# Hybrid decoder layer on one core: the bias table is stored once per head, and the queries of a block are kept last one first

## Chip, cores and metric

The kernel runs on one core of a Trainium2 chip. The metric is the device time of one execution in microseconds, as the median of several runs; lower is better.

## What is computed

One layer of a decoder with 256 tokens of width 2048, all in float32. The parts that matter here are the attention heads: 6 differential heads (A), 4 block heads (B) and 6 dilated heads (C), each of width 128. Every logit gets a bias that depends on the distance between query and key alone, through a table of 32 buckets and 16 heads:

```
def rel_bias(table, dist):
    return jnp.moveaxis(table.astype(jnp.float32)[t5_bucket(dist)], -1, 0)
...
        dist = qpos[:, None] - kpos[None, :]
        s = jnp.einsum('bhcqd,bhckd->bhcqk', qi, kt).astype(jnp.float32) * scale
        s = s + rel_bias(table, dist)[None, :, None]
        s = jnp.where(dist >= 0, s, NEG_INF)
        p = jax.nn.softmax(s, axis=-1)
```

After the heads come an output projection, a cross attention to 256 memory tokens, and a gated feed-forward part of width 5632. The weights are about 222 MB (212 pieces of 1 MB), each read once.

## The kernel before

**Weights and products.** Each weight matrix is cut into pieces of 1 MB (`raw`, four buffers). SyncE's queue issues the load of a piece (`load`, line 126) as soon as VectorE is done with the buffer that it takes. A piece is worked in two halves: ScalarE casts a half to the rounded type float32r (`split_hi`, line 141, tile `hi`), VectorE takes the difference (`split_lo`, line 148, tile `lo`), and TensorE multiplies with both. The split runs four halves ahead of the products. There are two kinds of products: `wstat_chunk` (lines 264 and 268) has the weights stationary, `astat_chunk` (lines 307 to 309) has the tokens stationary.

**Order.** The order on every engine is written out by hand. The program counts halves; `before(i, f)` and `after(i, f)` hang other work on half i, ahead of VectorE's split of it or behind TensorE's products of it. Heads run in this way beside the products: scores, softmax, transposes and the product with the values are spread over some ten halves. The last lines of the kernel walk through all halves and issue what hangs on them.

**The bias.** `setup_small`, hung on half 14, makes on TensorE and VectorE one row of 384 values for each head (tile `s`, called `rev` in the code): the bias of the distances 255, 254 and so on. GpSimd's queue then stores it to DRAM (line 967), in the tensor `bias_dram`. `load_bias` (line 355) reads for a head a tile `bias` of 128 queries by 256 keys, in which each query's row is shifted by one against the row above. It is issued six halves ahead of the head's scores, on SyncE's queue, between loads of weights. `biased` (line 399) adds it to the scores.

**Queries.** `merge_to` (line 336) writes the transposed queries and keys of a head (tile `qk`) with the factor of the norm, `copied` (line 417) takes the transposed probabilities out of PSUM (tile `pt`) for the product with the values.

Of the kernel before, what the change touches and what calls it, by code (L numbers as in the profile page):

```python
# [11 lines left out]
F32 = mybir.dt.float32  # L12
F32R = mybir.dt.float32r
AF = mybir.ActivationFunctionType
ALU = mybir.AluOpType
AX = mybir.AxisListType

P = 128
D = 2048
S = 256  # L20
NT = 2
KD = D // P
# [18 lines left out]

# First distance of each relative-position bucket that distances 0..255 reach.
BUCKET_AT = list(range(17)) + [22, 30, 40, 54, 73, 99, 134, 182, 246]
RL = 384


def bias_constants():
    """By shape alone: the bucket of the distance 255 - i, one-hot, and what each head group adds to it."""
    dist = 255 - np.arange(RL)
    bucket = np.searchsorted(np.array(BUCKET_AT), np.maximum(dist, 0), side="right") - 1  # L50
    onehot = np.zeros((NBUCK, RL), np.float32)
    onehot[bucket, np.arange(RL)] = dist >= 0
    add = np.full((NH, RL), NEG, np.float32)
    add[: HA + HB, dist >= 0] = 0.0
    times = (dist <= 128).astype(int) + (dist % 4 == 0) + (dist % 16 == 0)
    seen = (dist >= 0) & (times > 0)
    add[HA + HB :, seen] = np.log(times[seen].astype(np.float64)).astype(np.float32)
    return onehot, add
# [3 lines left out]
def trunk(ctx, tc, x, mem, w_in, w_out, g_mix, diff_lambda, diff_subln, rel_bias_table, g_cross, g_mem,  # L62
# [25 lines left out]
    def any_tile():  # L88
        """All the banks in turn, where nothing but products needs them."""
        turn[0] += 1  # L90
        return (acc_tile if turn[0] % 8 < NACC else at_tile)()
# [3 lines left out]

    # ---------------------------------------------------------------- loads of weights
    # A piece is 1 MB of a weight matrix, one 8 KB row in each partition; it is split into its two
    # float32r parts in two halves.
    class Piece:
# [51 lines left out]

    # What runs beside the products: `before` what the vector engine does ahead of a half's work, `after`
    # the rest. A value that goes from one engine to another is mostly picked up a half later, so that no
    # engine waits in its queue.
    pre, post = {}, {}
# [11 lines left out]

    # ---------------------------------------------------------------- constants
    ident = cst.tile([P, P], F32, name="ident")
# [5 lines left out]

    # ---------------------------------------------------------------- norms
    def rstd_of(ss, n, width, r=None):
        """(ss / n + eps) ** -0.5 of [P, width] sums of squares."""
        ms = small(width, f"ms{width}")
        DVE.tensor_scalar(ms, ss, 1.0 / n, EPS, op0=ALU.mult, op1=ALU.add)  # L180
        if r is None:
            r = small(width, f"rstd{width}")
        POOL.tensor_tensor(r, ms, mhalf.to_broadcast([P, width]) if width > 1 else mhalf, op=ALU.pow)
        return r

    def put_steps(src, g, dst, c):
        """Transposes 256 columns, src(t) of 128 tokens, of a norm's input, times the gain, into the two
        float32r parts of dst[:, 2c:2c+2, :]; the products take the rows' factor afterwards."""
        st = {}

        def turn():
            st["p"] = at_tile()
            for j in range(2):
                for t in range(NT):
                    o = j * S + t * P
                    PE.transpose(st["p"][:, o:o + P], src(t)[:, j * P:(j + 1) * P], ident)  # L196

        def high():
            for j in range(2):
                k = 2 * c + j  # L200
                ACT.activation(dst()[:, k, :S], st["p"][:, j * S:(j + 1) * S], AF.Copy, scale=gT[:, g, k:k + 1])

        def low():
            for j in range(2):
                k = 2 * c + j
                DVE.scalar_tensor_tensor(dst()[:, k, S:], st["p"][:, j * S:(j + 1) * S], gT[:, g, k:k + 1],
                                         dst()[:, k, :S].bitcast(F32), op0=ALU.mult, op1=ALU.subtract)

        return turn, high, low
# [12 lines left out]
    def norm_factors(i, key, ss):  # L222
        """The norm's factor of each token, from sums [P, (t c)] of squares: in a column and along rows."""
        st = {}
# [24 lines left out]

    # ---------------------------------------------------------------- products  # L250
    def wstat_chunk(w, col0, ncol, src, evac, rows=KD, bank=acc_tile):
        """(src @ w[:, col0:col0+512]).T, 128 columns to a bank: [hi x hi + lo x hi | hi x lo]."""
        accs = [None] * 4
# [34 lines left out]
    def astat_chunk(w, col0, ncol, src, evac, korder):  # L288
        """src @ w[:, col0:col0+ncol], 128 tokens to a bank; korder are blocks of 128 rows of w."""
        accs = [None] * NT  # L290
# [34 lines left out]
    def merge(a):  # L325
        """a[:, :256] + a[:, 256:]."""
        t = tmp.tile([P, S], F32, tag="mg", name="mg", bufs=4)
        ACT.copy(t, a[:, S:])
        DVE.tensor_tensor(t, a[:, :S], t, op=ALU.add)  # L329
        return t  # L330

    def merge_to(n, place, a, scale, key, wait=0):
        """The n-th of four: place() = scale * rows' factor * merge(a)."""
        m = merge(a)
        before(cur[0] + 1 + wait + n // 2,
               lambda: DVE.scalar_tensor_tensor(place(), m, scale, rrow[key], op0=ALU.mult, op1=ALU.mult))

# [3 lines left out]

    # ---------------------------------------------------------------- attention
    qT, kT, vN = {}, {}, {}
# [3 lines left out]
    lam = small(1, "lam", 1)  # L347
    bias_dram = dram.tile([NH, P, RL], F32, name="bias_dram")
    BT = {}

    def load_bias(h):
        BT[h] = pools["att"].tile([P, S], F32, tag="bias", name="bias", bufs=4)
        src = bass.AP(tensor=bias_dram.tensor, offset=bias_dram.offset + h * P * RL + 127,
                      ap=[[RL - 1, P], [1, S]])
        SP.dma_start(BT[h], src)

# [9 lines left out]
    def products(out, a, b, first=True, last=True):  # L366
        """out += a.T @ b, of [high, low] float32r parts."""
        for i, (u, w) in enumerate(((0, 0), (0, 1), (1, 0))):
            PE.matmul(out, a[u], b[w], start=first and i == 0, stop=last and i == 2)  # L369

    def spare(n):
        """Room in the heads' outputs that only the last group fills."""
        return mixed["t"][:, HA + 2 * (n % 2):HA + 2 * (n % 2) + 2, :]
# [20 lines left out]
    def biased(sp, b, nm):  # L394
        """scores + bias of both query blocks into SBUF; minus their maxima into nm."""
        s = pools["att"].tile([P, RL], F32, tag="s", name="s", bufs=3)
# [11 lines left out]
    def transposed(s):  # L408
        """P.T of [q0 x k0 | q1 x k0 | q1 x k1]."""
        pt = at_tile()  # L410
        for j in range(3):
            PE.transpose(pt[:, j * P:(j + 1) * P], s[:, j * P:(j + 1) * P], ident)  # L412
        return pt

    def copied(pt):
        t = pools["att"].tile([P, RL], F32, tag="pt", name="pt", bufs=4)
        ACT.copy(t, pt[:, :3 * P])
        return t
# [163 lines left out]

    # ---------------------------------------------------------------- the program, piece by piece
    # Projections of one group of heads.
    def group(col0, nheads, h0, tag, qscale):
        def put(dst, h, scale):
            def f(n, a):
                dst[h] = pools["att"].tile([P, S], F32, tag="qk", name="qk", bufs=16)
                merge_to(n, lambda: dst[h], a, scale, "x", 5 if cur[0] < KD // 2 else 0)
            return f  # L590
# [40 lines left out]

    # Output projection, with the residual; the memory's norm in between.
    ss1 = small(8, "ss1", 1)
# [68 lines left out]

    # One buffer: the heads' outputs, the transposed weights and the values, each in two parts.
    def new_cross():
# [69 lines left out]

    # Down projection: all banks, every weight once.
    outs = {}
# [88 lines left out]

    # ---------------------------------------------------------------- start
    g4 = pools["att"].tile([P, S], F32, tag="on", name="on", bufs=2)[:4 * KD, :P]
# [41 lines left out]

    # The tensor engine's clock rises with steady work: it turns the identity until the first loads are there.  # L910
    warm = acc_tile()
# [40 lines left out]
    def setup_small():  # L952
# [13 lines left out]
        DVE.tensor_tensor(rev, pr[:NH, :RL], badd, op=ALU.add)  # L966
        POOL.dma_start(bias_dram, rev[:, None, :].to_broadcast([NH, P, RL]))
        pc = at_tile()
# [54 lines left out]
```

## Time and profile before

| what | value |
|---|---|
| median of 3 runs | 1282.57 us (1282.16 to 1284.3) |
| span of the profiled execution, first to last instruction | 1281.3 us |
| mean granted clock of TensorE | 0.991 |
| busy: TensorE, VectorE, ScalarE, GpSimd | 1253.5, 809.3, 629.7, 18.2 us |
| moved by DMA | 236.33 MB, 184 GB/s in the mean |

Of the profiled execution only its span is known, which is 1.3 us shorter than the median. A busy time counts an engine's instructions and none of its waits. The ends of matmuls are modelled, so the distances between their starts tell more than their lengths. The DMA share is the busy share of the sixteen DMA engines in the mean, whatever they move in that time; it can come out slightly above 1.

### The profile page before, as it was taken

What the parts mean: (1) busy time and instruction counts of PE and PEld (TensorE: products, weight loads), DVE (VectorE), ACT (ScalarE), POOL (GpSimd) and SP (SyncE); (2) the same over time, 40 slices, a digit from 0 to 9 for tenths busy, and PEclk for the clock granted to TensorE, in tenths of its full rate; (3) what the DMA queues carried; (4) which work ended last, traced back from release to release, by engine and by line L of the source; (5) the groups of instructions that cost most, each with busy time, mean ns of one, the idle gap of its engine ahead of it and who ended that gap; (6) DMA issues with size and microseconds to landing.
All of it is one profiled execution on the core that took longest, in us unless ns stands there. A gap on an engine that the chain in (4) does not pass through costs nothing.

```text
span 1281.3 us, 17348 instructions
## 1 busy us (share of the span) xinstructions
PE 1253.5 (98%) x6784; PEld 1070.4 (84%) x6784; DVE 809.3 (63%) x1304; ACT 629.7 (49%) x1017; POOL 18.2 (1%) x31
## 2 busy tenths in 40 slices
PE   8969999999999999999999999999999999999997
PEld 7857888888888889888888888888888888888885
DVE  5625677567555577677677677767767765445455
ACT  5514565556455555654444444445444444444444
POOL 1000000000000000000000000000000000000000
PEclk9988999999999999999999999999999999999998
DMA  9697554555456554555555555555555555555541
GB/s 326 206 152 234 173 176 163 188 178 172 158 166 241 174 165 135 214 178 175 200 185 182 204 178 192 178 200 183 184 204 177 190 197 179 182 197 185 180 161 66
DMA packets 106465, 236.33 MB, mean 184 GB/s; under 512 B 4283, under 2 KB 15130, under 8 KB 100624
## 3 DMA queue, kind: packets, MB, share of 16 engines
q1 hardware_dynamic: 105296, 231.75, 53.0%
q0 software_dynamic: 1056, 3.47, 2.4%
q8 instruction: 53, 0.87, 0.3%
q14 instruction: 28, 0.23, 0.1%
q10 hardware_dynamic: 32, 0.01, 0.0%
HBM read 229.97 MB, written 5.24 MB: 184 GB/s over the span
## 4 chain that ended last, share of the span: by engine, by line
issue 58%; PE 36%; DMA 4%; DVE 1%; SPq 0%; POOL 0%; ACT 0%; DVEq 0%; POOLq 0%; ACTq 0%
PE acc L264 10%; PE acc L307 6%; PE acc L308 6%; PE acc L309 6%; PE acc L268 5%; DMA raw<-in_w_in 3%; DMA xbig<-in_x 1%; PE at L369 1%; PE at L196 1%; PE at L388 0%; PE at L412 0%; PE at L440 0%; SPq L136 0%; DVE lo L148 0%; PE at L441 0%
## 5 line engine op out<-in xcount | busy, mean ns | idle before, releaser
L148 DVE TENSOR_TENSOR lo<-raw,hi 128x1024 fp32r<-128x1024 f32 x424 | 518.3, 1224 | 400.2 <-ACT hi L141 399.3
L141 ACT CAST hi<-raw 128x1024 fp32r<-128x1024 f32 x424 | 443.9, 1049 | 487.0 <-PE acc L264 244.5
L264 PE MATMUL acc<-hT,hi 128*128 128x512 f32 x1520 | 539.1, 396 | 0.0
L268 PE MATMUL acc<-hT,lo 128*128 128x256 f32 x1520 | 421.1, 279 | 0.0
L264 PEld LDWEIGHTS acc<-hT,hi 128*128 128x128 f32 x1520 | 284.7, 187 | 66.9
L268 PEld LDWEIGHTS acc<-hT,lo 128*128 128x128 f32 x1520 | 283.9, 188 | 0.3
L264 PE MATMUL at<-hT,hi 128*128 128x512 f32 x528 | 188.6, 393 | 0.0
L307 PE MATMUL acc<-hi,hT 128*128 128x512 f32 (+1 forms) x384 | 140.7, 366 | 13.7 <-DVE mg L329 13.7
L268 PE MATMUL at<-hT,lo 128*128 128x256 f32 x528 | 147.3, 279 | 0.0
L308 PE MATMUL acc<-lo,hT 128*128 128x512 f32 (+1 forms) x384 | 138.3, 360 | 0.0
L309 PE MATMUL acc<-hi,hT 128*128 128x512 f32 (+1 forms) x384 | 138.3, 360 | 0.0
L264 PEld LDWEIGHTS at<-hT,hi 128*128 128x128 f32 x528 | 98.9, 187 | 23.7
L268 PEld LDWEIGHTS at<-hT,lo 128*128 128x128 f32 x528 | 98.9, 187 | 0.0
L307 PEld LDWEIGHTS acc<-hi,hT 128*128 128x128 f32 x384 | 73.0, 190 | 25.0 <-DVE mg L329 14.1
L797 PE MATMUL acc<-lo,ah 128*128 128x512 f32 x220 | 87.2, 396 | 0.0
L796 PE MATMUL acc<-hi,ah 128*128 128x512 f32 x220 | 87.2, 396 | 0.0
L798 PE MATMUL acc<-hi,al 128*128 128x512 f32 x220 | 87.2, 396 | 0.0
L309 PEld LDWEIGHTS acc<-hi,hT 128*128 128x128 f32 x384 | 73.0, 190 | 12.0
L308 PEld LDWEIGHTS acc<-lo,hT 128*128 128x128 f32 x384 | 73.1, 190 | 10.7
L798 PE MATMUL at<-hi,al 128*128 128x512 f32 x132 | 52.3, 396 | 0.0
L796 PE MATMUL at<-hi,ah 128*128 128x512 f32 x132 | 52.3, 396 | 0.0
L797 PE MATMUL at<-lo,ah 128*128 128x512 f32 x132 | 52.3, 396 | 0.0
(159 smaller groups left out, 920.1 us busy)
## 6 DMA issues: line engine op xcount, KB each, us to landing
raw<-in_w_up SPq DMA_DIRECT2D x88, 1024.0 KB, 4.9
raw<-in_w_in SPq DMA_DIRECT2D x45, 1024.0 KB, 5.2
raw<-in_w_down SPq DMA_DIRECT2D x44, 1024.0 KB, 4.9
raw<-in_w_out SPq DMA_DIRECT2D x12, 1024.0 KB, 5.5
raw<-in_w_ckv SPq DMA_DIRECT2D x8, 1024.0 KB, 5.2
raw<-in_w_out SPq DMA_DIRECT2D x8, 512.0 KB, 5.0
raw<-in_w_cq SPq DMA_DIRECT2D x4, 1024.0 KB, 5.3
raw<-in_w_co SPq DMA_DIRECT2D x4, 1024.0 KB, 5.2
```

The source lines that it names most:

```text
L141: ACT.copy(hi, p.raw[:, h * HALF:(h + 1) * HALF])
L148: DVE.tensor_tensor(lo, p.raw[:, h * HALF:(h + 1) * HALF], hi.bitcast(F32), op=ALU.subtract)
L196: PE.transpose(st["p"][:, o:o + P], src(t)[:, j * P:(j + 1) * P], ident)
L264: PE.matmul(accs[n], hi[:, j, n * P:(n + 1) * P], src()[:, k, :], start=(k == 0), stop=False)
L268: PE.matmul(accs[n][:, :S], lo[:, j, n * P:(n + 1) * P], src()[:, k, :S], start=False, stop=(k == rows - 1))
L307: PE.matmul(o, xh, hi[:, j, :], start=(i == 0), stop=False)
L308: PE.matmul(o, xh, lo[:, j, :], start=False, stop=False)
L309: PE.matmul(o, xl, hi[:, j, :], start=False, stop=(i == len(korder) - 1))
L369: PE.matmul(out, a[u], b[w], start=first and i == 0, stop=last and i == 2)
L796: PE.matmul(o, ah, wh, start=(k == 0), stop=False)
L797: PE.matmul(o, ah, wl, start=False, stop=False)
L798: PE.matmul(o, al, wh, start=False, stop=(k == KF - 1))
```

## The change

The tensor `bias_dram` has one row for each head, not one for each query of each head, and the store writes that row once. A row of 384 values is the same for all queries but for its shift. A load can step forwards by one value from partition to partition, where the tile of before steps back by one. So partition p of the tile `bias` now belongs to query 127 - p of its block, and the queries are put in that order: `merge_to` reads its two inputs of each block of 128 backwards when it writes queries, and `copied` reads the transposed probabilities of each block backwards, which restores the order. Keys and values stay as they are. The comments that were removed are left out here.

```
     def merge_to(n, place, a, scale, key, wait=0, order=lambda a: a):
         m = merge(a)
         before(cur[0] + 1 + wait + n // 2,
-               lambda: DVE.scalar_tensor_tensor(place(), m, scale, rrow[key], op0=ALU.mult, op1=ALU.mult))
+               lambda: DVE.scalar_tensor_tensor(place(), order(m), scale, order(rrow[key]), op0=ALU.mult,
+                                                op1=ALU.mult))
...
+    def turned(a):
+        return a.rearrange("p (t n) -> p t n", t=2)[:, :, ::-1]
...
-    bias_dram = dram.tile([NH, P, RL], F32, name="bias_dram")
+    bias_dram = dram.tile([NH, RL], F32, name="bias_dram")
...
-        src = bass.AP(tensor=bias_dram.tensor, offset=bias_dram.offset + h * P * RL + 127,
-                      ap=[[RL - 1, P], [1, S]])
+        src = bass.AP(tensor=bias_dram.tensor, offset=bias_dram.offset + h * RL, ap=[[1, P], [1, S]])
         SP.dma_start(BT[h], src)
...
         t = pools["att"].tile([P, RL], F32, tag="pt", name="pt", bufs=4)
-        ACT.copy(t, pt[:, :3 * P])
+        ACT.copy(t.rearrange("p (j n) -> p j n", j=3), pt[:, :3 * P].rearrange("p (j n) -> p j n", j=3)[:, :, ::-1])
...
+                if dst is qT:
+                    merge_to(n, lambda: t.rearrange("p (t n) -> p t n", t=2), a, scale, "x", late, turned)
+                else:
+                    merge_to(n, lambda: t, a, scale, "x", late)
...
-        POOL.dma_start(bias_dram, rev[:, None, :].to_broadcast([NH, P, RL]))
+        POOL.dma_start(bias_dram, rev)
```

No instruction is added, taken away or moved on TensorE, VectorE, ScalarE and SyncE. On GpSimd, whose rows around the store follow, with those that begin with - for before and + for after, the store alone has another shape: the numbers are rows and values of the transfer.

```order
 L183 TENSOR_TENSOR rcol_x<-ms_501,mhalf 128x2
-L967 DMA bias_dram<-s 2048x1x384
+L977 DMA bias_dram<-s 16x384
 L183 TENSOR_TENSOR rstd_1363<-ms_1361,mhalf 128x2
 L183 TENSOR_TENSOR rstd_1596<-ms_1594,mhalf 128x2
```

The transfer goes from 2048 rows to 16 and stands where it stood; later lines of the file have moved by ten.

## Rows read from the trace of the kernel before

**Rows 1.** The page: the span, and busy time, share and instructions of the engines.

```profile
span 1281.3 us, 17348 instructions
...
PE 1253.5 (98%) x6784; PEld 1070.4 (84%) x6784; DVE 809.3 (63%) x1304; ACT 629.7 (49%) x1017; POOL 18.2 (1%) x31
```

**Rows 2.** Long stretches: length, busy time of each engine, granted clock, DMA share, GB/s.

```profile
160.00:320.00 160.00, 160.00 (x951) 139.50 (x950) 111.21 (x277) 94.43 (x211) 3.45 (x5) 1.00 0.53 176
...
112.00:1264.00 1152.00, 1151.97 (x6250) 985.14 (x6250) 742.92 (x1198) 571.23 (x919) 7.29 (x9) 1.00 0.53 181
```

**Rows 3.** All waits of TensorE: total us, times, longest us.

```profile
PE acc L307 <- DVE mg L329: 13.7, 1, 13.7
PE at L196 <- DMA xbig<-in_x: 3.9, 5, 1.4
PE acc L915 <- POOL mhalf L172: 1.3, 1, 1.3
```

**Rows 4.** The longest wait of another engine in 80 to 98 us.

```profile
ACT hi L141 <- DMA raw<-in_w_in: 18.7, 1, 18.7
```

**Rows 5.** The chain that ended last: start, us, what.

```profile
59.67 34.41 DMA raw<-in_w_in
```

**Rows 6.** DMA in 40 to 56 us: packets, MB, share of 16 engines.

```profile
q1 hardware_dynamic: 1354, 2.70, 52.6%
```

**Rows 7.** The same in 56 to 98 us; then an issue, us to landing.

```profile
q0 software_dynamic: 704, 3.15, 71.3%
q1 hardware_dynamic: 1951, 3.86, 24.0%
...
bias_dram<-s POOLq DMA_DIRECT2D x1, 3072.0 KB, 35.9
```

**Rows 8.** Stretches of 8 us, with the columns of rows 2.

```profile
64.00:72.00 8.00, 8.00 (x48) 6.99 (x47) 3.68 (x3) 2.80 (x4) 0.00 (x0) 1.00 0.97 104
...
80.00:88.00 8.00, 4.31 (x23) 3.34 (x22) 0.00 (x0) 0.00 (x0) 0.00 (x0) 0.93 1.01 137
88.00:96.00 8.00, 0.00 (x0) 0.00 (x0) 0.74 (x1) 1.82 (x2) 0.00 (x0) 0.50 1.00 231
96.00:104.00 8.00, 5.99 (x14) 4.74 (x15) 6.65 (x12) 3.25 (x7) 0.00 (x0) 0.50 1.07 365
```

**Rows 9.** DMA issues of the whole span: count, KB each, median us to landing.

```profile
raw<-in_w_down SPq DMA_DIRECT2D x44, 1024.0 KB, 4.9
...
gfin<-in_g_final SPq DMA_DIRECT2D x1, 1024.0 KB, 6.9
...
s<-in_biasadd POOLq DMA_DIRECT2D x1, 24.0 KB, 7.1
```

**Rows 10.** TensorE in order of time around the gap: start, us, instruction.

```profile
83.21 0.39 PE L309 MATMUL acc<-hi,hT 128*128 128x512 f32 x1
...
83.91 0.40 PE L309 MATMUL acc<-hi,hT 128*128 128x512 f32 x1
...
98.01 0.80 PE L307 MATMUL acc<-hi,hT 128*128 128x512 f32 x1 [13.70 <-DVE mg L329]
...
104.32 0.39 PE L307 MATMUL acc<-hi,hT 128*128 128x512 f32 x1
```

**Rows 11.** The stretch behind the gap, with the columns of rows 2.

```profile
98.00:104.30 6.30, 6.29 (x15) 4.97 (x16) 4.65 (x9) 1.25 (x2) 0.00 (x0) 0.52 1.08 355
```

**Rows 12.** The tile `bias`: ns least/median/most, first and last start.

```profile
L399 DVE CUSTOM_DVE_ANT_0 s<-at,bias x44: 281/356/422, 137.1 to 326.2; 128x128 f32<-128x128 f32 x22, 128x256 f32<-128x256 f32 x22
L355 SPq DMA_DIRECT2D bias<-bias_dram x16: 338/498/901, 110.8 to 302.6; - x16
```

**Rows 13.** The lines 336, 417 and 971, with the columns of rows 12.

```profile
L336 DVE SCALAR_TENSOR_TENSOR qk<-mg,rrow x32: 415/418/422, 49.5 to 306.0; 128x256 f32<-128x256 f32 x32
L417 ACT COPY pt<-at x16: 466/474/492, 146.8 to 337.3; 128x384 f32<-128x384 f32 x16
L971 DVE COPY convT<-at x1: 449/449/449, 58.1 to 58.1; 128x176 f32<-128x176 f32 x1
```

More of the change, by code (lines that the diff above doesn't have):

```diff
@@ L330, in merge, with merge_to @@
         return t
-    def merge_to(n, place, a, scale, key, wait=0):
+    def turned(a):
+        return a.rearrange("p (t n) -> p t n", t=2)[:, :, ::-1]
+    def merge_to(n, place, a, scale, key, wait=0, order=lambda a: a):
         m = merge(a)
         before(cur[0] + 1 + wait + n // 2,
-               lambda: DVE.scalar_tensor_tensor(place(), m, scale, rrow[key], op0=ALU.mult, op1=ALU.mult))
+               lambda: DVE.scalar_tensor_tensor(place(), order(m), scale, order(rrow[key]), op0=ALU.mult,
+                                                op1=ALU.mult))
     def high_low(hi, lo, x, scale=1.0):
@@ L587, in f @@
             def f(n, a):
-                dst[h] = pools["att"].tile([P, S], F32, tag="qk", name="qk", bufs=16)
-                merge_to(n, lambda: dst[h], a, scale, "x", 5 if cur[0] < KD // 2 else 0)
+                dst[h] = t = pools["att"].tile([P, S], F32, tag="qk", name="qk", bufs=16)
+                late = 5 if cur[0] < KD // 2 else 0
+                if dst is qT:
+                    merge_to(n, lambda: t.rearrange("p (t n) -> p t n", t=2), a, scale, "x", late, turned)
+                else:
+                    merge_to(n, lambda: t, a, scale, "x", late)
             return f
```

## Prediction

> **What bounds the kernel now.** I read the busy times first: TensorE is busy 1253.5 of 1281.3 us, and no other engine passes 63% [rows 1]. So only what TensorE executes, or what makes it stand still, sets the time. From 112 to 1264 us it is busy 1151.97 of 1152.00 us at a granted clock of 1.00 [rows 2]: nothing there is to be won without fewer or shorter matmuls, and nothing that another engine does there is on the path as long as it is not late.
>
> The list of waits has one large entry for TensorE: 13.7 us once, at line 307 [rows 3]. The releaser named is VectorE's `mg`; but that instruction merely stood last in VectorE's queue, and what was late is found further back: ScalarE's cast of a weight piece waited 18.7 us for the load of `raw` from `in_w_in` [rows 4], and VectorE's split waits behind that cast. The chain of the end shows the load itself: issued at 59.67 us, landed 34.41 us later [rows 5], where pieces of 1 MB elsewhere land in 4.9 us [rows 9].
>
> What filled the DMA engines is in the queues' shares of 56 to 98 us: the software queue, on which GpSimd stores `bias_dram`, held 71.3% of the sixteen engines' time, the weights' hardware queue only 24.0% [rows 7]. The store is 3072 KB and took 35.9 us to land. Before it the engines were not short: from 40 to 56 us the weights needed 52.6% of them [rows 6]. In the stretches of 8 us the whole story is seen [rows 8]: the DMA share goes to 1.00 while the traffic falls to 104 GB/s, TensorE's work ends in 80 to 88 us, the next stretch has none, and the granted clock is 0.50 there and in the one after.
>
> **The change, part by part.** *The store shrinks.* It writes 16 rows of 384 values in place of 2048, so 24 KB in place of 3072 KB; the lists of instructions differ on no engine except in this one transfer's shape. Its old cost on the engines: 71.3% of 16 x 42 us is 479 engine-us, 0.234 us for each of 2048 rows. Sixteen rows at that price are 3.7 engine-us: 0.23 us if all engines share them, 3.7 us if one engine has them all. The nearest row from the other side is the 24 KB load of `in_biasadd` on the same queue, which took 7.1 us to land in the crowded start [rows 9]. TensorE went on for 24.5 us after the first starved load was issued (59.67 to 84.14 us), on pieces already loaded and already split. Against that cover 0.23, 3.7 and 7.1 us are all hidden: I put the new store at 0, and the stall disappears whole.
>
> What the stall is worth I count from TensorE's own instructions [rows 10]. In steady work three matmuls of 512 columns start in 0.70 us (83.21 to 83.91), 0.234 us each. The last before the gap starts at 83.91, so the next was due at 84.14; it starts at 98.01. That is 13.87 us of standing. After it 15 matmuls start before the one at 104.32 [rows 11], 0.42 us apart in the mean, the pace of the granted clock of 0.50 (1.2 of 2.4 GHz): 6.31 us where 15 x 0.234 = 3.51 would do, so 2.80 us more. Together **16.7 us** (as a check: 104.32 - 83.91 = 20.41 us for 16 matmuls that need 3.75).
>
> The clock part can be had in another way, so I weigh it. By the rows the clock was 0.93, 0.50 and 0.50 in the three stretches of 8 us from 80 to 104 us [rows 8], so at half for 1.1 + 8 + 8 = 17.1 us, but TensorE has matmuls only in its last 6.3 us, and only these are lengthened. The Trainium skill, "TensorE: Matmul & The Clock Gate", section "Terms", prices throttling as the throttled time times one minus the clock ratio: an estimate by that page is 17.1 x 0.5 = 8.6 us in place of 2.8, and a sum of 22.4 us. The rows speak against using it here, since idle time costs the same at either clock; I keep 2.8.
>
> *The stall has no second home, if weights keep landing.* The pieces that follow are used at one in 6.0 us (212 pieces in 1281 us, a half in 3.0 us [rows 1]) and land in about 5 [rows 9]; after 98 us TensorE never waits again [rows 2, 3], and all that follows is the same list of instructions moved 16.7 us earlier.
>
> *The reads of the table.* Each of 16 loads of `bias` still takes 128 rows of 1 KB, but now all 128 lie in the same 1.5 KB of DRAM, one value apart. No row shows this for `bias`; the nearest is the load of `gfin`, which gives every partition the same 8 KB: 6.9 us for 1 MB, against 4.9 us for a piece of `in_w_down` of the same size with rows of its own [rows 9]. So from no change to 1.4 times: 5.0 to 7.0 us. The first load is issued at 110.8 us and its first reader starts at 137.1 [rows 12]: 26.3 us of cover. I put it at 0.
>
> *Reading backwards.* Sixteen products `qk` on VectorE (line 336, 418 ns, 256 values) and sixteen copies `pt` on ScalarE (line 417, 474 ns, 384 values) now walk each block from its end. No row has a negative step. The lower bound is no change. The upper I take from strided work: the copy of `convT`, whose writes are four values apart, takes 449 ns for 176 values, 2.55 ns each, where line 336 takes 1.63 [rows 13]. That is 0.92 ns more: 0.24 us for each product and 0.35 us for each copy, 3.8 and 5.6 us in all. These engines are busy 111 and 94 of 160 us in 160 to 320 us [rows 2], and the parts of a head are a half piece (3.0 us) or more apart in the queue. I put it at 0; were the cover gone, 9.4 us would come back. The Trainium skill, "Vector Engine (DVE) Microarchitecture Reference", section "Measured stream behaviour on trn2", measures up to 2.51 ns a value for small non-adjacent steps and says that a negative step was not measured; an estimate by it is 0.37 us for each product, hidden as well.
>
> **Sum.** Profiled execution: span 1281.3 - 16.7 = 1264.6 us. The median of the runs is 1282.57, 1.3 us above that span; with the same distance the forecast is **1265.9 us**.
>
> **Rivals.**
> *The clock gives back more.* The half clock's cost is 8.6 us, not 2.8, as if the engine would have used all of its 17.1 us: 1282.57 - 22.4 = 1260.2 us. For it is only that one cannot see what the clock would do without the gap; against it are the starts counted above. The Trainium skill, "TensorE: Matmul & The Clock Gate", section "Terms", would have it so. 3 in 100.
> *The backwards reads come to the path.* TensorE's transposes and products of the heads wait for `qk` and `pt`, at the worst for all of 9.4 us: 1275.3 us. For: VectorE's work of a head comes in bursts. Against: TensorE waits for neither anywhere in the profile of before [rows 3]. 3 in 100.
> *The stall stays.* If the weights were late by themselves, the store is innocent and the time is 1282.6. Against: 71.3% in its queue, and 52.6% of use just ahead of it. 2 in 100.
> *Slower.* The loads of `bias` crowd on one spot of DRAM and hold the engines. They come every 12.8 us (15 steps from 110.8 to 302.6 [rows 12]), and the weights use 53% [rows 2], so 6.0 us are free in each step. With the cover of 24.5 us, the gain is gone and 2.6 us more lost when each load holds all engines for 6.0 + (24.5 + 16.7 + 2.6) / 16 = 8.7 us; at 10 us it is 16 x 4.0 - 24.5 - 16.7 = 22.8 us worse, 1305 us. Against: `gfin` reads eight times as many bytes from one spot in 6.9 us from issue to landing. 2 in 100.
>
> **Numbers.** The forecast has 90 in 100. Its range takes 0.4 us below and 1.7 above from the spread of the runs (1282.16 to 1284.3), another 2.5 us below for starts near the gap that are modelled or missing, and 2.4 above for a quarter of the backwards price: 1263 to 1270 us, which leaves out the rivals, together 1 in 10. A change of 0.2% (2.6 us) is about what can be told from none. Faster 0.96 (forecast, clock, backwards), same 0.02 (stall stays), slower 0.02.
>
> **What the profile will show.** Right: no wait of TensorE over 2 us after the start; granted clock 1.00 in every slice from the third on; some 3.1 MB less on the software queue; pieces landing in 5 us between 59 and 95 us; the first matmul at line 307 about 0.23 us behind the one ahead of it. Wrong: `bias` landing in over 8 us; TensorE waiting at the transposes or scores of the heads; lines 336 and 417 much over 0.66 and 0.83 us; or a gap still between 80 and 100 us.

## The result, and the profile after

The changed kernel takes 1266.41 us (median of 4 runs, 1266.02 to 1266.92) against 1282.62 us for the kernel before: a ratio of 0.9872 with a 95% interval of 0.9858 to 0.9886. That is 16.2 us by the medians; the spans of the two profiled executions differ by 16.5 us. The forecast was 1265.9 us.

The page of the changed kernel, span, busy times, granted clock and DMA share in 40 slices:

```profile
span 1264.8 us, 17348 instructions
...
PE 1250.7 (99%) x6784; PEld 1068.6 (84%) x6784; DVE 809.0 (64%) x1304; ACT 630.2 (50%) x1017; POOL 17.7 (1%) x31
...
PEclk9999999999999999999999999999999999999998
DMA  9655554555465454555555565565655555555541
```

The busy times of VectorE and ScalarE are the same to 0.5 us [rows 1]; TensorE is 2.8 us less busy, which is what its matmuls at half clock had been longer. Only the last slice, where the work ends, is below nine tenths of the clock.

All waits of TensorE after, as in [rows 3]:

```profile
PE at L196 <- DMA xbig<-in_x: 3.9, 5, 2.0
PE acc L925 <- POOL mhalf L172: 1.4, 1, 1.4
```

The 13.7 us are gone and nothing has come in their place; the two small waits of the start are as before. The stretches that held the gap [rows 8] have full work at full clock, with the DMA engines busy for 0.45 to 0.75 of the time:

```profile
64.00:72.00 8.00, 8.00 (x48) 6.96 (x47) 3.74 (x4) 2.80 (x4) 0.00 (x0) 1.00 0.45 148
...
80.00:88.00 8.00, 8.00 (x40) 6.64 (x39) 6.08 (x11) 4.45 (x7) 0.00 (x0) 1.00 0.59 195
88.00:96.00 8.00, 8.00 (x36) 6.44 (x35) 3.23 (x4) 3.16 (x3) 0.00 (x0) 1.00 0.51 148
96.00:104.00 8.00, 8.00 (x35) 6.43 (x35) 3.25 (x4) 3.15 (x3) 0.00 (x0) 1.00 0.75 261
```

The DMA queues in 56 to 98 us after, to be laid beside [rows 7], and the issues there with the time to landing:

```profile
q1 hardware_dynamic: 5217, 8.33, 60.6%
...
q0 software_dynamic: 32, 0.02, 0.2%
...
raw<-in_w_in SPq DMA_DIRECT2D x7, 1024.0 KB, 5.2
bias<-bias_dram SPq DMA_DIRECT2D x1, 128.0 KB, 5.0
bias_dram<-s POOLq DMA_DIRECT2D x1, 24.0 KB, 1.8
```

The store lands in 1.8 us in place of 35.9, and the pieces beside it land in 5.2 us. At the place of the old gap, where the second bank of the first value product begins, TensorE goes on 0.24 us after the matmul ahead of it:

```profile
84.12 0.40 PE L309 MATMUL acc<-hi,hT 128*128 128x512 f32 x1
84.36 0.39 PE L307 MATMUL acc<-hi,hT 128*128 128x512 f32 x1
```

### The profile page after: what moved, and what is told of

Read it like the earlier page. It is cut to its first block, busy times and chain, and to the rows that moved or that the text cites. A ratio compares the mean times of both kernels' runs of the same rounds, so it can differ in the third digit from the quotient of the medians.

```text
span 1264.8 us, 17348 instructions
## 1 busy us (share of the span) xinstructions
PE 1250.7 (99%) x6784; PEld 1068.6 (84%) x6784; DVE 809.0 (64%) x1304; ACT 630.2 (50%) x1017; POOL 17.7 (1%) x31
## 4 chain that ended last, share of the span: by engine, by line
issue 58%; PE 39%; DMA 1%; SPq 0%; DVE 0%; POOL 0%; ACT 0%; DVEq 0%; POOLq 0%; ACTq 0%
PE acc L264 11%; PE acc L307 6%; PE acc L309 6%; PE acc L308 6%; PE acc L268 6%; DMA xbig<-in_x 1%; PE at L375 1%; PE at L196 1%; PE at L394 0%; PE at L418 0%; PE at L446 0%; SPq L136 0%; PE at L447 0%; SPq L885 0%; POOL raw L820 0%
```

## Experiments

Each is compared with the kernel before, run beside it; where a small difference matters the interval is given.

**The old store with the queries turned.** One part of the change is undone. The load of a head begins at the head's first row, as it must in the larger tensor (left out here); it still steps forwards.

```
-    bias_dram = dram.tile([NH, RL], F32, name="bias_dram")
+    bias_dram = dram.tile([NH, 128, RL], F32, name="bias_dram")
...
-        POOL.dma_start(bias_dram, rev)
+        POOL.dma_start(bias_dram, rev[:, None, :].to_broadcast([NH, 128, RL]))
```

> The changed kernel with the queries turned, but with the old store of 128 equal rows per head (3072 KB). If the store alone made the time: 1282.6 us within 2, the store landing in about 36 us, one wait of TensorE of 13.7 us near 84 us and half clock behind it. If the backwards order has a price of its own, up to 9.4 us more than that; if the order of the queries (and not the store) gave the gain, 1266 us. Lines 340 and 423 take 418 and 472 ns as in the changed kernel either way.

Measured: 1282.56 us, ratio 1.0001 (0.9992 to 1.0011). The store lands in 36.1 us, lines 340 and 423 take 422 and 472 ns in the median, and TensorE's list of waits has its large entry again:

```profile
PE acc L307 <- DVE mg L329: 14.1, 1, 14.1
```

So the whole gain is the store's; the order of the queries alone gives nothing and costs nothing, to within the 0.1% of that interval.

**Plain order with the small store.** Here the backwards reads are taken out, and each query gets another one's bias.

```
-                    merge_to(n, lambda: t.rearrange("p (t n) -> p t n", t=2), a, scale, "x", late, turned)
+                    merge_to(n, lambda: t, a, scale, "x", late)
...
-        ACT.copy(t.rearrange("p (j n) -> p j n", j=3), pt[:, :3 * P].rearrange("p (j n) -> p j n", j=3)[:, :, ::-1])
+        ACT.copy(t, pt[:, :3 * P])
```

> The changed kernel with the small store and the new loads, but queries in plain order: the two backwards reads are taken out, so each query gets the bias of another one. If backwards reads cost nothing: 1266.4 us within 1, lines for qk and pt at 418 and 472 ns. If they had a hidden price on the path: 1260 to 1265 us.

Measured: 1266.41 us, the same median as the changed kernel. The two lines first in the changed kernel (nanoseconds least, median, most):

```profile
L340 DVE SCALAR_TENSOR_TENSOR qk<-mg,rrow x32: 411/418/422, 49.7 to 289.5; 128x256 f32<-128x256 f32 x32
L423 ACT COPY pt<-at x16: 470/472/494, 130.3 to 320.9; 128x384 f32<-128x384 f32 x16
```

and then in this one:

```profile
L340 DVE SCALAR_TENSOR_TENSOR qk<-mg,rrow x32: 415/419/423, 49.5 to 289.3; 128x256 f32<-128x256 f32 x32
L423 ACT COPY pt<-at x16: 469/472/491, 130.1 to 320.7; 128x384 f32<-128x384 f32 x16
```

Half of the 32 products and all 16 copies read backwards in the first and none in the second, and the medians differ by 1 ns at most, less than the 4 ns by which line 340 differs between executions: a step of minus one in float32 costs nothing on these engines here.

**Less of the store.** The two kernels store 96 and 64 equal rows for each head, in place of 1 (and of 128 before); but for the tensor's shape and the load's start, which follow, they are the changed kernel. With 96:

```
-        POOL.dma_start(bias_dram, rev)
+        POOL.dma_start(bias_dram, rev[:, None, :].to_broadcast([NH, 96, RL]))
```

> The changed kernel with 96 equal rows per head stored (2304 KB). If the DMA engines' time is the cause, the store lands in about 27 us, the first starved piece with it at 85 to 86 us, and TensorE stands some 5 us in place of 13.9; with 0 to 2.8 us for the clock that is 1271 to 1275 us. If any big store costs the same stall (a fixed wait, or its start): 1282 us. If the cover of 24.5 us held in full against the 27 us: 2 to 3 us of standing, 1269.

> The changed kernel with 64 equal rows per head stored (1536 KB). By the engines' time the store lands in about 18 us, under the cover of 24.5 us: no wait of TensorE, clock 1.00, 1266.4 us within 1. If the loss goes in proportion to the bytes: half of 16.7 us, 1275 us.

Measured: 1275.22 us with 96 rows, 1266.41 us with 64. The stores landed in 27.5 and 18.6 us, as the engines' time has it. With 64 rows TensorE waits nowhere near the place, so the loss does not go with the bytes: it begins past a threshold, which lies between 18.6 and 27.5 us to landing. With 96 rows it stands:

```profile
83.65 0.40 PE L309 MATMUL acc<-hi,hT 128*128 128x512 f32 x1
87.19 1.99 ACT L141 CAST hi<-raw 128x1024 fp32r<-128x1024 f32 x2 [11.96 <-DMA raw<-in_w_in]
88.27 2.36 DVE L148 TENSOR_TENSOR lo<-raw,hi 128x1024 fp32r<-128x1024 f32 x2 [11.79 <-ACT hi L141]
89.09 1.19 ACT L328 COPY mg<-acc 128x256 f32<-128x256 f32 x4
...
90.55 1.41 DVE L329 TENSOR_TENSOR mg<-acc,mg 128x256 f32<-128x256 f32 x4
91.02 0.79 PE L307 MATMUL acc<-hi,hT 128*128 128x512 f32 x1 [6.97 <-DVE mg L329]
...
95.26 0.39 PE L308 MATMUL acc<-lo,hT 128*128 128x512 f32 x1
```

That is 7.1 us of standing where I expected some 5. The piece, issued at 59.4 us, lands 27.7 us later, at 87.1, where I expected it at 85 to 86; from there a cast, two splits and the first of the four sums `mg` still go ahead of TensorE's first matmul, 3.8 us (87.19 to 91.02). The ten matmuls that start ahead of the one at 95.26 take 4.24 us, where 2.34 would do at full clock; 7.1 and 1.9 make 9.0 us, against 8.8 by the medians.

**A free bank for the waiting product.** The rows above name not the weights but `mg`. In the kernel before, only the second bank of PSUM of the first value product is taken from the other ring, which is idle there.

```
-                        accs[t] = acc_tile()
+                        accs[t] = (at_tile if cur[0] == 24 and t else acc_tile)()
```

> The kernel before, with one edit: the second bank of PSUM of the first value product (half 24) comes from the other, idle ring of banks, so that TensorE needn't wait until VectorE has emptied a bank of the product ahead. If TensorE stood for that bank, as the list of waits names it, it goes on with the 18 matmuls whose halves are split (4.2 us), and starts again at about 96.5 us when the next half is split: 5.7 us less, 1276.9 us, the wait then named by the weights' tiles. If it stood for the weights, as my prediction read it: 1282.6 us.

Measured: 1276.71 us, ratio 0.9957 (0.9940 to 0.9974). TensorE goes on until the split halves are used up:

```profile
83.91 0.39 PE L307 MATMUL at<-hi,hT 128*128 128x512 f32 x1
...
87.89 0.39 PE L309 MATMUL at<-hi,hT 128*128 128x512 f32 x1
94.23 1.99 ACT L141 CAST hi<-raw 128x1024 fp32r<-128x1024 f32 x2 [18.99 <-DMA raw<-in_w_in]
95.31 2.36 DVE L148 TENSOR_TENSOR lo<-raw,hi 128x1024 fp32r<-128x1024 f32 x2 [18.81 <-ACT hi L141]
95.33 0.80 PE L307 MATMUL acc<-hi,hT 128*128 128x512 f32 x1 [7.05 <-ACT hi L141]
```

The 18 matmuls run ahead of the gap, and the wait is now 7.05 us and for the weights. So in the kernel before TensorE stood for the bank: its emptying was queued, on ScalarE and VectorE, behind casts and splits that waited for the late piece, while one and a half split halves lay ready. The rows of the kernel before show that queue; TensorE's matmul at 98.01 us [rows 10] starts when the first of the four sums `mg` is done:

```profile
94.18 1.99 ACT L141 CAST hi<-raw 128x1024 fp32r<-128x1024 f32 x2 [18.70 <-DMA raw<-in_w_in]
95.26 2.36 DVE L148 TENSOR_TENSOR lo<-raw,hi 128x1024 fp32r<-128x1024 f32 x2 [18.52 <-ACT hi L141]
96.08 1.19 ACT L328 COPY mg<-acc 128x256 f32<-128x256 f32 x4
...
97.54 1.41 DVE L329 TENSOR_TENSOR mg<-acc,mg 128x256 f32<-128x256 f32 x4
```

**Work in the gap.** Transposes of the identity are put where TensorE of the kernel before stands, to see what the half clock costs.

```
+                    if cur[0] == 24 and t == 0:
+                        fill = at_tile()
+                        for _ in range(210):
+                            PE.transpose(fill[:, :P], ident, ident)
```

> The kernel before, with 210 additional transposes of the identity (about 12 us, their result is not used) at the place where TensorE stands still. If only the matmuls behind the gap are lengthened by the half clock: the clock stays at 1.00 and the time is 1282.6 - 2.8 = 1279.8 us. If the half clock costs half of its 17.1 us: 1274.0 us. If the transposes take longer than the gap: more than 1282.6.

Measured: 1289.98 us. The transposes took 22.85 us (84.80 to 107.65), longer than the gap, so the third case came and the time by itself does not part the first two; but they kept the clock up, as the stretches behind the rows of TensorE show:

```profile
84.80 17.41 PE L313 MATMUL at<-ident 128*128 128x128 f32 x158
...
107.65 0.47 PE L307 MATMUL acc<-hi,hT 128*128 128x512 f32 x1
```

```profile
88.00:96.00 8.00, 8.00 (x76) 8.00 (x75) 0.00 (x0) 0.00 (x0) 0.00 (x0) 1.00 0.99 204
96.00:104.00 8.00, 8.00 (x75) 8.00 (x74) 6.16 (x11) 4.04 (x7) 0.00 (x0) 1.00 1.07 372
```

In place of the gap and the half clock there are 22.85 us. If those two cost 13.87 + 2.80 us, the span grows by 6.2 us; if they cost 13.87 + 8.6, by 0.4. It grew by 6.9 (1288.2 against 1281.3), of which 0.66 us had come up before the place was reached (the first value matmul starts at 83.41, in the kernel before at 82.75). That leaves 6.2; by the medians the time grew by 7.3 us.

> The filler again, with 115 transposes in place of 210, since 210 took 22.85 us (0.109 us each): 12.5 us, inside the gap of 13.9 us. If only the matmuls behind the gap are lengthened by the half clock: clock 1.00 through the gap, 1282.6 - 2.8 = 1279.8 us. If the half clock costs half of its 17.1 us: 1274.0 us. If the clock is of no account: 1282.6 us.

Measured: 1282.56 us in the median of ten, 1281.63 without the tenth, ratio 0.9994 (0.9985 to 1.0004): inconclusive. In the profiled execution, one of 1283.82 us, the late piece came some 2 us later than before (its cast starts at 96.21 us, not at 94.18), so the filler ended 2.48 us too soon and the clock fell once more for a short time:

```profile
84.84 12.72 PE L313 MATMUL at<-ident 128*128 128x128 f32 x115
100.03 0.51 PE L307 MATMUL acc<-hi,hT 128*128 128x512 f32 x1 [2.48 <-DVE mg L333]
```

Five executions took 1280.29 to 1281.63 us, near the first theory, and four 1283.48 to 1284.08. The tenth took 2530.35 us, for which I have no explanation.

**What made the store slow.** In the changed kernel a further store of 3072 KB, whose result is not used, is put behind the small one: the same number of rows of the same length on the same queue, but read from 128 partitions.

```
+    wide_dram = dram.tile([P, NH, RL], F32, name="wide_dram")
...
+        POOL.dma_start(wide_dram, xbig[:, 0:1, :RL].to_broadcast([P, NH, RL]))
```

> The changed kernel with an additional store of 3072 KB at the same place and on the same queue, of the same 2048 rows of 1536 bytes, but read from all 128 partitions (16 copies of one row each; the result is not used). If the old store was slow because all rows came from 16 partitions: it lands in 8 to 12 us, no wait of TensorE, 1266 to 1267 us. If such rows written by this queue are slow whatever their source: 36 us to landing and 1282 us or more.

Measured: 1267.37 us in two runs (1266.62 to 1268.13). It landed in 17.6 us, later than the 8 to 12 expected, and TensorE did not wait. The software queue's packets, bytes and share of 56 to 100 us:

```profile
q0 software_dynamic: 736, 3.17, 17.7%
```

That is 17.7% of 16 x 44 us for 736 packets, 0.17 us each; before, 71.3% of 16 x 42 us for 704 packets was 0.68 us [rows 7]. Read from 16 partitions, the same bytes were four times as costly to the DMA engines as from 128. The two stores differ in one thing more: each row is read 128 times in the old one and 16 times in this one. No run parts the two, so that the few partitions are the reason, and not the repeats, is not shown.

The last one moves the store of the kernel before from GpSimd's software queue to ScalarE's hardware queue.

```
-        POOL.dma_start(bias_dram, rev[:, None, :].to_broadcast([NH, P, RL]))
+        ACT.dma_start(bias_dram, rev[:, None, :].to_broadcast([NH, P, RL]))
```

> The kernel before, with the store of 3072 KB issued from ScalarE's hardware queue in place of GpSimd's software queue. If the source or the rows are slow: about 36 us to landing and 1282.6 us within 2. If the software queue is what is slow: under 12 us to landing, no wait of TensorE and 1266 us.

Measured: 1274.31 us in two runs, between the two expectations. The store is as slow (35.4 us to landing), so its slowness is not the software queue's; yet the first starved piece lands in 24.4 us in place of 34.4, and the wait is 4.6 us. The queues of 76 to 84 us, in the kernel before and then in this one, with packets, bytes and share:

```profile
q0 software_dynamic: 163, 0.75, 89.5%
q1 hardware_dynamic: 162, 0.33, 10.7%
```

```profile
q10 hardware_dynamic: 478, 0.73, 71.1%
q1 hardware_dynamic: 477, 0.96, 30.9%
```

In both, the two queues take turns packet by packet here (163 to 162, 478 to 477). The hardware queue's packets of the store are shorter (0.73 MB in 478 of them against 0.75 MB in 163), so here a packet of weights has its turn three times as often. The Trainium skill, "DMA: Bandwidth & Descriptors", section "Queues, rings and completion order", says that an engine goes round the queues at packet granularity; these rows agree. Earlier the turns are not seen: from 66 to 74 us the weights had 64 packets to the store's 165 on the software queue, and none to 506 on the hardware queue. What held them back there stays open, and so does how much of the shorter wait the packets' length explains.

## Why the prediction was right, and where it was not

**The cause.** That the store of the table starved the weights is shown: with the small store the gap is gone, with the old store it is back whatever the order of the queries (1282.56 us, within 0.1% of the kernel before), and with 96 rows it is smaller. It was the store's cost to the DMA engines and not its size, since 3072 KB at a quarter of the cost for each packet leave no wait of TensorE.

**The size.** 13.87 us of standing and 2.80 us at half clock, 16.7 us, against 16.5 measured by the spans. The weighing of the clock's part, 2.8 us and not 8.6, holds: the result itself is 16.2 us, not 22.4, and the long filler gives the same.

**The new store at nothing.** Right: it landed in 1.8 us, and even 18.6 us (64 rows) were hidden.

**Whose wait it was.** This step failed, though the sum did not depend on it. I wrote that `mg` "merely stood last in VectorE's queue" and that the cover of 24.5 us was pieces loaded and split. The bank experiment showed that TensorE did wait for `mg`, for a bank of PSUM, and that 4.2 us of matmuls, already loaded and split, lay unused behind that; with the bank free the wait was 7.05 us in place of 13.7. The sum came out all the same because the small store takes away the late piece, and with it both waits. The list of waits had been right in what it named; the late load was the cause one step further back.

**The loads of the table.** Right at the lower bound: 5.1 us to landing in the median, against 5.0 before, though all 128 rows now lie in 1.5 KB. So the rival that was slower did not come.

**Reading backwards.** Right at the lower bound; the upper one, from writes four values apart, was not reached in any part. The remark of the Trainium skill that a negative step was not measured stands in another section of the page named, "Performance modes — why throughput varies by op and dtype"; here such reads took 418 and 472 ns, as forward ones did.

**No second home.** Right: TensorE has no wait over 2.0 us after. One sign was put too strongly: the last slice is below full clock after, as it was before, since TensorE's work has ended there.

## What to carry to other kernels

When an engine that should always be busy has one long wait, look at what the DMA engines did in the time ahead of it, by queue: a share of 1.00 with little traffic (104 GB/s) was here a transfer that is costly in its shape, and the kernel's loads paid for it. It cost nothing until it outlasted the loads' lead, so its price counts from a threshold on and is not in proportion to its bytes. Work that frees a buffer should not be queued behind work that waits for a load, since that makes the lead shorter than the buffers suggest.

## What the runs showed of the hardware that I had not expected

The same 3 MB in rows of 1536 bytes took the DMA engines 0.68 us for each packet when they were read from 16 partitions, each row 128 times, and 0.17 us from 128 partitions, each row 16 times. From 76 to 84 us a slow store left the weights 0.33 MB on the software queue, with packets of some 4.6 KB, and 0.96 MB on a hardware queue, with packets of 1.5 KB, although it landed equally late (35.9 and 35.4 us). Reads with a step of minus one in float32 took as long as forward ones on VectorE (418 and 419 ns) and ScalarE (472 ns both).
